# Setting the order of instructions anew: a matmul's weight load counted apart, other priorities

## The chip, the core and the metric

The kernel runs on one core of one Trainium2 chip. The metric is device time in microseconds (us) of one execution. A core has engines with instruction queues of their own that run side by side and wait for one another through semaphores: TensorE (PE, with its weight loads listed apart as PEld), VectorE (DVE), ScalarE (ACT), GpSimd (POOL), and SyncE (SP), which here does nothing but issue DMAs. Within one queue instructions run in the order in which they were written. That order is what the change touches.

## The reference

One layer of an encoder trunk, for a prompt of 1024 tokens and a sample of 32 tokens, all in float32, model width 1024:

- `u = rmsnorm(h) @ w_in` gives q, k, v and a gate for two groups (A, B) of 8 heads of width 64 each.
- Group A is softmax attention with a relative-position bias, over the query's own chunk of 64 positions and the 8 chunks before it. Group B is "stick-breaking" attention: weight `exp(log_sigmoid(z) + sum of log_sigmoid(-z) over the later keys)`, strictly causal. The sample's queries also see a cache of 512 keys and values.
- `y = concat(oA * silu(gA), oB * silu(gB)) @ w_out`, then `h = h + rmsnorm(y)`, then `h = h + sigmoid(h @ w_ple_gate) * (p @ w_ple)`.
- Outputs are both results and the new keys and values.

## The kernel before

**Work.** Each float32 operand of a matrix product is split into a high and a low part (names ending in h and l), and a product is three matmuls: high by high, high by low, low by high. `mm_*` are the input projections: 32 column blocks (q, k, v and the gate g, groups A and B, four pairs of heads), each in 3 chunks of 352 tokens and 24 matmuls per chunk. `S*` are attention scores, `ptw*` transposes of the attention weights on PE, `PV*` weights times values; a name with a small s (`SsB`, `PVsB`, `KhsB`) belongs to the sample. `ple` is `p @ w_ple`. `o0P` to `o3P` and `g0P` to `g3P` are the two closing 1024x1024 products, done by a scheme of seven block products; `o` and `g` with 64 weight columns are the sample's share of them.

**Stages.** Stage 0 is the norm and the first projections; stages 1 to 8 each mix the attention of one pair of heads with the projections of the next pair (stage 8: the gates); stage 9 is the late part of `ple`; stages 10 to 13 are the closing products.

**Buffers.** A column block's raw weights come by DMA into tiles with the tag `wr`, of which there are 4 (two per block); ACT casts them to `wh`, POOL subtracts to get `wl`. The same 4 rooms with tag `wr` also hold the sample's keys and values (`Kh`, `Kl`, `Vh`, `Vl`), so a weight load can have to wait until the sample's matmuls have read them. SP issues all DMAs from one queue.

**What sets the order.** The program does not write its instructions as the code runs. `Recorder` keeps each one as an `Op` with what it depends on; at the end `emit` (called on the last line of `stream_step`) asks `order` for one sequence and writes it. `order` runs `simulate`, a list scheduler: each engine takes, of the ops that are ready, the one with the lowest rank, and a time that `cost` estimates from the op's size passes. After each run, `latest` goes backward from the end and gives each op a due time, the latest moment at which it could start. The next run ranks by due time. In the last of the 9 passes an op's own priority is added:

```
            out, end = self.simulate(lambda o: (o.key[0], o.index + last * o.shift, o.index) if o.eng == "PE" and not PE_LATEST else (0, o.due + last * 10 * o.shift, o.index))
```

The priority, `o.shift`, is the sum of two table entries: `AHEAD_OF[engine, kind]` and `AHEAD_AT[stage, engine, kind]`, where the kind is the first letters of the written tile's name up to a digit, an A, a B or an underscore (`wr_kA2` gives `wr`, `SsB0` gives `Ss`, `wlS1o2` gives `wlS`). It is multiplied by 10 and added to a due time in ns: +100 puts an op 1 us later in the ranking, -100 1 us earlier. It changes only the order in which ready ops are taken, and no data.

For PE, `cost` before gives a transpose 109 ns (62 ns for at most 64 rows) and a matmul the larger of 109 ns and 2.5 + 0.449 ns for each streamed column. `MARGIN` (400 ns) is what the scheduler adds to whatever PE waits for from another engine. For a DMA it adds `DMA_START` (1850 ns), the transfer at `DMA_RATE` or by its pieces, and `DMA_MARGIN` (2100 ns).

All engine calls pass through one helper, so nearly every row of the profile has the line 781; tiles' names tell them apart.

Of the kernel before, what the change touches and what calls it, by code (L numbers as in the profile page):

```python
# [28 lines left out]
    ('ACT', ''): -307, ('ACT', 'L'): -414, ('ACT', 'Qfs'): -110, ('ACT', 'Qhs'): -859,  # L29
    ('ACT', 'S'): -381, ('ACT', 'be'): 32, ('ACT', 'g'): 244, ('ACT', 'gT'): -473,  # L30
    ('ACT', 'hnh'): 1092, ('ACT', 'kd'): 363, ('ACT', 'newh'): -483, ('ACT', 'o'): -50,
    ('ACT', 'om'): -5, ('ACT', 'p'): -1128, ('ACT', 'sq'): 108, ('ACT', 'stk'): 127,
    ('ACT', 'stq'): -682, ('ACT', 'wh'): -79, ('ACT', 'whS'): -249, ('ACT', 'xS'): -955,
    ('ACT', 'xb'): -149, ('ACT', 'yb'): -199, ('DVE', ''): -1363, ('DVE', 'Kl'): 290,
    ('DVE', 'L'): 377, ('DVE', 'R'): 818, ('DVE', 'S'): 18, ('DVE', 'Ss'): -133,
    ('DVE', 'Vh'): -402, ('DVE', 'cc'): 216, ('DVE', 'diags'): -224, ('DVE', 'gT'): 610,
    ('DVE', 'h'): 1157, ('DVE', 'hnl'): 253, ('DVE', 'lg'): -586, ('DVE', 'newl'): 326,
    ('DVE', 'o'): 347, ('DVE', 'ot'): -72, ('DVE', 'over'): 1049, ('DVE', 'sgg'): 302,
# [3 lines left out]
    ('PE', 'ptxs'): 7, ('POOL', 'be'): 315, ('POOL', 'bias'): 960, ('POOL', 'g'): 573,  # L42
    ('POOL', 'ksS'): 1098, ('POOL', 'om'): -712, ('POOL', 'r'): -536, ('POOL', 'sgg'): 1213,
# [5 lines left out]
}  # L49
AHEAD_AT = {  # L50
    (0, 'ACT', 'hnh'): -902, (0, 'ACT', 'pleo'): 783, (0, 'ACT', 'sq'): 26, (0, 'ACT', 'v'): -215,
    (0, 'PE', 'mm'): -297, (0, 'PE', 'ple'): 252, (0, 'POOL', 'wl'): -634, (0, 'SP', 'wpr'): 528,
    (0, 'SP', 'wr'): -232, (0, 'SP', 'x'): -74, (1, 'ACT', 'ot'): -442, (1, 'ACT', 'wTh'): 589,
    (1, 'ACT', 'wh'): 43, (1, 'DVE', 'S'): 928, (1, 'DVE', 'om'): 258, (1, 'DVE', 'wTl'): 279,
    (1, 'PE', 'S'): -86, (1, 'SP', 'sum'): -1097, (2, 'ACT', 'L'): 674, (2, 'ACT', 'be'): -112,
    (2, 'ACT', 'ot'): -548, (2, 'ACT', 'vt'): 555, (2, 'ACT', 'wTh'): 152, (2, 'DVE', 'om'): 60,
    (2, 'DVE', 'vt'): 389, (2, 'PE', 'S'): 43, (2, 'SP', 'o'): 677, (2, 'SP', 'sum'): 621,
    (3, 'ACT', 'Qfs'): 130, (3, 'ACT', 'stq'): 1238, (3, 'ACT', 'wh'): 323, (3, 'DVE', 'L'): -248,
    (3, 'DVE', 'Vh'): 390, (3, 'DVE', 'Vl'): 233, (3, 'DVE', 'diags'): 564, (3, 'DVE', 'om'): 40,
    (3, 'DVE', 'ot'): 169, (3, 'DVE', 'over'): 620, (3, 'DVE', 'vt'): 997, (3, 'DVE', 'vx'): 1005,  # L60
# [3 lines left out]
    (4, 'ACT', 'stq'): 92, (4, 'ACT', 'wTh'): -49, (4, 'DVE', 'Kl'): 168, (4, 'DVE', 'S'): 37,  # L64
    (4, 'DVE', 'Vl'): 530, (4, 'DVE', 'newl'): -393, (4, 'DVE', 'om'): -78, (4, 'DVE', 'v'): 323,
# [3 lines left out]
    (5, 'ACT', 'stv'): 620, (5, 'ACT', 'wTh'): 828, (5, 'ACT', 'wh'): 111, (5, 'DVE', 'S'): 706,  # L69
# [13 lines left out]
    (8, 'ACT', 'om'): -708, (8, 'ACT', 'ot'): -106, (8, 'ACT', 'sgg'): -442, (8, 'ACT', 'wTh'): 312,  # L83
    (8, 'DVE', 'Kcs'): -163, (8, 'DVE', 'Kl'): 236, (8, 'DVE', 'S'): 304, (8, 'DVE', 'Vl'): 1322,
# [7 lines left out]
    (11, 'ACT', 'g'): 533, (11, 'ACT', 'junk'): 705, (11, 'ACT', 'x'): 430, (11, 'ACT', 'xS'): 262,
    (11, 'DVE', 'h'): -403, (11, 'PE', 'o'): -12, (12, 'ACT', 'gT'): -495, (12, 'ACT', 'x'): -260,
    (12, 'DVE', 'gT'): -1415, (12, 'DVE', 'gj'): 887, (12, 'POOL', 's'): -859, (12, 'SP', 'hh'): 748,
    (13, 'ACT', 'x'): -379, (13, 'DVE', 'S'): 55, (13, 'DVE', 'cc'): 684, (13, 'DVE', 'wlS'): -69,
    (13, 'PE', 'g'): 217,
# [148 lines left out]
class Op:  # L245
    __slots__ = ("pieces", "eng", "what", "args", "kw", "key", "busy", "late", "ready", "left", "after", "at", "size", "shared", "table", "start", "shift", "due", "size_", "index", "users", "tiles", "old")
# [12 lines left out]
BANKS = {'mm': 1, 'S': 2, 'T': 1, 'PV': 1}  # L259
PASSES = 9  # L260
PE_LATEST = True


class Pool:
    def __init__(self, rec, stack, tc, kw):
        self.rec, self.kw, self.stack, self.tc, self.real = rec, kw, stack, tc, None
        self.psum = kw.get("space") == bass.MemoryType.PSUM
        self.tags, self.ops, self.opened = {}, [], None

    def open(self):  # L270
        self.real = self.stack.enter_context(self.tc.tile_pool(**self.kw))

# [146 lines left out]
class Recorder:  # L419
# [149 lines left out]
    def latest(self, end):  # L569
# [16 lines left out]
        while done < len(self.ops):  # L586
# [19 lines left out]
            if e != "CTL":  # L606
                free[e] = ends[o.index]
# [1669 lines left out]
```

## Time and profile before

| what | value |
|---|---|
| median of 3 runs | 767.75 us (766.9 to 767.9) |
| profiled execution: span from first to last instruction | 765.7 us |
| what lies around the span: median less span | about 2.0 us |
| PE busy | 755.8 us (99%), 4410 matmuls |
| PEld (weight loads) busy | 699.5 us (91%) |
| DVE busy | 615.7 us (80%) |
| ACT busy | 525.1 us (69%) |
| POOL busy | 447.7 us (58%) |
| DMA | 173.73 MB, mean 227 GB/s |
| granted TensorE clock, mean | 1.000 |

The profile gives no separate total time for the profiled execution, only its span; the 2.0 us is the difference between the runs' median and it. PE's busy time is the union of its matmuls from start to modelled end, and neighbours overlap, so a mean duration in a row is longer than what a matmul takes from the one before it to the one after it. That pace is read from the chain of waits, where "x24" with a length says how long 24 matmuls in a row took.

### The profile page before, as it was taken

How to read it: one execution, taken by the hardware profiler on the slowest of the kernel's cores; microseconds unless marked ns; L12 is line 12 of the kernel's file. 1: busy time of each engine (PE TensorE's matmuls, PEld its weight loads, DVE VectorE, ACT ScalarE, POOL GpSimd, SP SyncE). 2: the span in 40 equal slices, each digit the busy share in tenths (PEclk: the TensorE clock that was granted, in tenths of full speed). 3: DMA queues.
4: the chain of work that ended last, by engine and by line, in shares of the span. 5: the costliest groups of instructions: out<-in, count | busy, mean ns of one | idle time of the engine just before them, and what ended most of it. 6: DMA issues, size and time to landing. Idle time of an engine off the chain costs nothing.

```text
span 765.7 us, 14211 instructions
## 1 busy us (share of the span) xinstructions
PE 755.8 (99%) x4410; PEld 699.5 (91%) x4410; DVE 615.7 (80%) x1067; ACT 525.1 (69%) x1122; POOL 447.7 (58%) x503
## 2 busy tenths in 40 slices
PE   9999999999999999999999999999999999999997
PEld 7999999999998999999999999999998877888786
DVE  7837878898879999989798898887455688988985
ACT  6647767787766768876977786764337877784561
POOL 5623626953257555566772566778552449698453
PEclk9999999999999999999999999999999999999999
DMA  8748888778878849988878889995798856868846
GB/s 305 238 132 208 240 192 261 211 198 232 218 194 233 226 119 241 257 247 254 228 195 250 219 215 229 247 271 159 240 288 271 264 185 203 325 180 256 296 144 204
DMA packets 202525, 173.73 MB, mean 227 GB/s; under 512 B 67009, under 2 KB 164649, under 8 KB 202450
## 3 DMA queue, kind: packets, MB, share of 16 engines
q1 hardware_dynamic: 202450, 172.83, 78.7%
q8 instruction: 35, 0.57, 0.3%
q14 instruction: 40, 0.33, 0.1%
HBM read 105.72 MB, written 58.91 MB: 215 GB/s over the span
## 4 chain that ended last, share of the span: by engine, by line
PE 86%; DMA 5%; DVE 3%; ACT 2%; issue 1%; SPq 1%; POOL 0%; ACTq 0%; DVEq 0%; POOLq 0%
PE mm_vA L781 6%; PE mm_kB L781 6%; PE mm_qA L781 6%; PE mm_gA L781 6%; PE mm_gB L781 6%; PE mm_kA L781 6%; PE mm_qB L781 5%; PE PVB L781 4%; PE SA L781 3%; PE ple L781 3%; PE SB L781 3%; PE PVA L781 3%; PE o3P L781 3%; PE o1P L781 3%; PE g1P L781 3%; PE g0P L781 3%
## 5 line engine op out<-in xcount | busy, mean ns | idle before, releaser
L781 POOL TENSOR_TENSOR be<-be 128x256 f32<-128x256 f32 (+8 forms) x66 | 84.7, 1290 | 47.6 <-ACT be L781 17.8
L781 DVE TENSOR_TENSOR_SCAN be<-be,SB 128x384 f32<-128x384 f32 (+5 forms) x96 | 91.8, 962 | 12.0 <-ACT be L781 5.6
L781 ACT ACTIVATE be<-SB 128x384 f32<-128x384 f32 (+5 forms) x192 | 85.2, 499 | 18.2 <-DVE be L781 9.1
L781 DVE TENSOR_TENSOR wTl<-be,wTh 128x640 fp32r<-128x640 f32 (+2 forms) x48 | 58.6, 1228 | 4.5 <-ACT wTh L781 3.6
L781 DVE STREAM_TRANSPOSE be<-be 128x640 f32<-128x640 f32 (+3 forms) x56 | 47.7, 865 | 5.4 <-DMA be<-in_cache_b_k_dram 2.7
L781 ACT ACTIVATE be<-be,statA 128x640 f32<-128x640 f32 (+3 forms) x64 | 44.4, 695 | 10.2 <-DVE statA L781 10.0
L781 ACT CAST wTh<-be 128x640 fp32r<-128x640 f32 (+2 forms) x48 | 37.5, 785 | 4.3 <-DMA be<-swapB 2.9
L781 POOL TENSOR_TENSOR gB<-gB,gB 128x256 f32<-128x256 f32 x32 | 26.4, 845 | 18.5 <-DMA gB<-in_w_ple_gate_dram 18.5
L781 POOL TENSOR_TENSOR oB<-oB,oB 128x256 f32<-128x256 f32 x32 | 26.3, 837 | 12.7 <-DMA oB<-in_w_out_dram 10.7
L781 PE MATMUL SB<-kdB,LB 128*128 128x384 f32 (+5 forms) x96 | 33.0, 348 | 0.0
L781 PE MATMUL SB<-klB,LB 128*128 128x384 f32 (+5 forms) x96 | 33.0, 345 | 0.0
L781 DVE CUSTOM_DVE_ANT_0 be<-SA,biasA 128x320 f32<-128x320 f32 (+2 forms) x64 | 29.4, 481 | 4.0 <-PE SA L781 3.1
L781 PE MATMUL SA<-kdA,LA 128*128 128x320 f32 (+2 forms) x96 | 30.5, 322 | 0.0
L781 PE MATMUL SA<-klA,LA 128*128 128x320 f32 (+2 forms) x96 | 30.1, 317 | 0.0
L781 ACT CAST wTh<-ptwB 128x512 fp32r<-128x512 f32 (+3 forms) x48 | 22.4, 485 | 10.2 <-PE PVB L781 5.6
L781 DVE TENSOR_TENSOR wTl<-ptwB,wTh 128x512 fp32r<-128x512 f32 (+3 forms) x48 | 25.2, 543 | 3.8 <-ACT wTh L781 3.6
L781 PE MATMUL ptwB<-ident,be 128*128 128x128 f32 x144 | 26.7, 273 | 1.1 <-DVE be L781 0.7
L781 POOL TENSOR_TENSOR klA<-stkA,kdA 64x1024 fp32r<-64x1024 f32 (+2 forms) x9 | 19.9, 2215 | 10.9 <-ACT kdA L781 10.8
L781 DVE TENSOR_TENSOR LA<-stqA,LA 64x1024 fp32r<-64x1024 f32 (+2 forms) x9 | 16.7, 1857 | 10.4 <-ACT LA L781 10.2
L781 DVE TENSOR_TENSOR wTl<-ptwA,wTh 128x128 fp32r<-128x128 f32 (+3 forms) x48 | 22.1, 480 | 3.6 <-ACT wTh L781 3.4
L781 POOL TENSOR_TENSOR h<-h,x 128x512 f32<-128x512 f32 (+1 forms) x18 | 23.4, 1320 | 1.3 <-DVE h L781 1.3
L781 PE MATMUL PVB<-wTh,v2B 128*128 128x512 f32 (+1 forms) x96 | 24.1, 344 | 0.0
(694 smaller groups left out, 2652.3 us busy)
## 6 DMA issues: line engine op xcount, KB each, us to landing
swapA<-be SPq DMA_DIRECT2D x24, 320.0 KB, 3.8
be<-swapA SPq DMA_DIRECT2D x96, 80.0 KB, 2.5
oB<-in_w_out_dram SPq DMA_DIRECT2D x16, 256.0 KB, 4.5
sum_dro<-oB SPq DMA_DIRECT2D x16, 256.0 KB, 3.2
gB<-in_w_ple_gate_dram SPq DMA_DIRECT2D x16, 256.0 KB, 4.3
sum_drg<-gB SPq DMA_DIRECT2D x16, 256.0 KB, 3.3
x<-in_x_prompt_dram SPq DMA_DIRECT2D x16, 256.0 KB, 4.5
h_dr<-h SPq DMA_DIRECT2D x8, 512.0 KB, 4.5
```

The costliest lines, as they stand in the source:

```text
L781: getattr(getattr(tc.nc, o.what[0]), o.what[1])(*args, **kw)
```

## The change

Three things change, all in what sets the order; no instruction's shape, operand or engine is edited.

1. The cost of a PE op is now its stream alone, 3.5 + 0.4444 ns per column (a transpose: per row of its input), with a weight load of its own, `ldw`, 0.84 ns per weight column (107.5 ns for 128). In `simulate` a matmul starts no earlier than its own `ldw` after the start of the matmul before it; `latest` does the same backward.
2. A rule is added that, when the load of the op picked would not be hidden, looks for another ready op. Its condition asks that the other op's rank be below the picked one's plus `REACH`, and `REACH` is -1e9, while ranks are due times in ns of a program under 1e6 ns long. The passes go from 9 to 7, and the first pass's rank is written as one number.
3. Both priority tables are replaced as a whole. Some entries of the old are gone, many are new, and the largest are larger: the extremes go from about 1500 to about 11800.

The diff, with the tables cut to entries that the prediction speaks of:

```diff
 AHEAD_OF = {
...
-    ('ACT', 'om'): -5, ('ACT', 'p'): -1128, ('ACT', 'sq'): 108, ('ACT', 'stk'): 127,
-    ('ACT', 'stq'): -682, ('ACT', 'wh'): -79, ('ACT', 'whS'): -249, ('ACT', 'xS'): -955,
...
-    ('PE', 'PVs'): -797, ('PE', 'S'): -13, ('PE', 'Ss'): 29, ('PE', 'g'): -731,
...
-    ('POOL', 'ug'): -306, ('POOL', 'w'): 1007, ('SP', 'Kcs'): -173, ('SP', 'be'): -36,
...
-    ('SP', 'swap'): -38, ('SP', 'to kt'): -281, ('SP', 'wpr'): -498, ('SP', 'wr'): -45,
...
+    ('DVE', 'wTl'): -113, ('DVE', 'wl'): -499, ('DVE', 'wlS'): 11801, ('PE', 'PVs'): -716,
+    ('PE', 'Ss'): -2427, ('PE', 'g'): 335, ('PE', 'o'): -60, ('PE', 'ptp'): 518, ('PE', 'ptxs'): -364,
...
+    ('SP', 'Kcs'): 293, ('SP', 'be'): -397, ('SP', 'g'): -1115, ('SP', 'hh'): -929, ('SP', 'kl'): -653,
...
 AHEAD_AT = {
...
-    (4, 'SP', 'Kcs'): 79, (4, 'SP', 'bias'): 406, (4, 'SP', 'o'): -439, (4, 'SP', 'vs'): -1467,
-    (4, 'SP', 'wr'): -239, (5, 'ACT', 'be'): -5, (5, 'ACT', 'om'): 123, (5, 'ACT', 'ot'): -1367,
...
-    (13, 'ACT', 'x'): -379, (13, 'DVE', 'S'): 55, (13, 'DVE', 'cc'): 684, (13, 'DVE', 'wlS'): -69,
...
+    (4, 'ACT', 'om'): 290, (4, 'ACT', 'vt'): 1686, (4, 'ACT', 'wTh'): 180, (4, 'ACT', 'wh'): 787,
...
+    (4, 'PE', 'S'): 8, (4, 'PE', 'ptw'): -9, (4, 'POOL', 'om'): 417, (4, 'SP', 'Kcs'): -805,
+    (4, 'SP', 'wr'): -789, (5, 'ACT', 'be'): 73, (5, 'ACT', 'stv'): -3106, (5, 'ACT', 'wTh'): 343,
...
+LOAD = 0.84
+REACH = -1e9
+SHORT = 70.0
...
-PASSES = 9
-PE_LATEST = True
+PASSES = 7
...
+        if eng == "PE":
+            o.ldw = LOAD * args[1].shape[-1]
...
             if method == "transpose":
-                return (109 if args[1].shape[0] > 64 else 62), 165
-            return max(109.0, 2.5 + 0.449 * args[2].free()) * (1 if args[2].buf.dtype == F32R else 4), 165
+                return 3.5 + 0.4444 * args[1].shape[0], 165
+            return (3.5 + 0.4444 * args[2].free()) * (1 if args[2].buf.dtype == F32R else 4), 165
...
-        out, end = self.simulate(lambda o: o.key)
+        out, end = self.simulate(lambda o: (0, o.key[0] * 1e7 + o.index, o.index))
...
-            out, end = self.simulate(lambda o: (o.key[0], o.index + last * o.shift, o.index) if o.eng == "PE" and not PE_LATEST else (0, o.due + last * 10 * o.shift, o.index))
+            out, end = self.simulate(lambda o: (0, o.due + last * 10 * o.shift, o.index))
...
             ends[o.index] = t + o.busy
+            if e == "PE":
+                ends[o.index] = max(ends[o.index], free[e] + loads)
+                loads = o.ldw
...
+            if e == "PE":
+                if o.ldw > begun[1]:
+                    held = [x for x in now[e] if self.ops[x[1]].ldw <= begun[1] and x[0][1] < ranks[o.index][1] + REACH]
+                elif o.ldw <= SHORT and o.busy > SHORT:
+                    held = [x for x in now[e] if self.ops[x[1]].busy <= SHORT < self.ops[x[1]].ldw and x[0][1] < ranks[o.index][1] + REACH]
+                else:
+                    held = []
+                if held:
...
+                t = max(t, begun[0] + o.ldw)
+                begun = t, o.busy
```

More of the change, by code (lines that the diff above doesn't have):

```diff
@@ L35 @@
[L35 to L38, printed above, removed]
[3 rows of a table removed]
-    ('PE', 'ptxs'): 7, ('POOL', 'be'): 315, ('POOL', 'bias'): 960, ('POOL', 'g'): 573,
-    ('POOL', 'ksS'): 1098, ('POOL', 'om'): -712, ('POOL', 'r'): -536, ('POOL', 'sgg'): 1213,
[5 rows of a table removed]
+    ('ACT', 'Qfs'): 1088, ('ACT', 'g'): 1834, ('ACT', 'h'): -1086, ('ACT', 'hnh'): -120,
@@ new lines @@
+    ('ACT', 'kd'): 429, ('ACT', 'newh'): 999, ('ACT', 'o'): -2101, ('ACT', 'oT'): -4320,
+    ('ACT', 'om'): -198, ('ACT', 'ot'): -399, ('ACT', 'p'): 4138, ('ACT', 'php'): -103,
+    ('ACT', 'pleo'): 91, ('ACT', 'sgg'): -2156, ('ACT', 'sq'): 118, ('ACT', 'stq'): -597,
+    ('ACT', 'stv'): 443, ('ACT', 'v'): -402, ('ACT', 'vt'): -1313, ('ACT', 'wTh'): -13,
+    ('ACT', 'x'): -289, ('ACT', 'xS'): -152, ('DVE', 'Kcs'): 317, ('DVE', 'Kl'): 3817,
+    ('DVE', 'L'): -68, ('DVE', 'Qls'): 1342, ('DVE', 'Vh'): 1210, ('DVE', 'diags'): 115,
@@ L49 @@
+    ('DVE', 'h'): 5659, ('DVE', 'om'): -23, ('DVE', 'ot'): -714, ('DVE', 'v'): 527, ('DVE', 'vt'): -530,
+    ('DVE', 'wTl'): -113, ('DVE', 'wl'): -499, ('DVE', 'wlS'): 11801, ('PE', 'PVs'): -716,
+    ('PE', 'Ss'): -2427, ('PE', 'g'): 335, ('PE', 'o'): -60, ('PE', 'ptp'): 518, ('PE', 'ptxs'): -364,
+    ('POOL', 'Qfs'): 1837, ('POOL', 'ksS'): -2511, ('POOL', 'sgg'): -2536, ('POOL', 'wl'): 301,
[4 rows of a table added]
 }
 AHEAD_AT = {
-    (0, 'ACT', 'hnh'): -902, (0, 'ACT', 'pleo'): 783, (0, 'ACT', 'sq'): 26, (0, 'ACT', 'v'): -215,
@@ L52 @@
[L52 to L57, printed above, removed]
@@ L92 @@
[L92 to L96 removed]
+    (0, 'ACT', 'sq'): -9, (0, 'DVE', 'hnl'): 9233, (0, 'PE', 'ple'): 7969, (0, 'POOL', 'ksS'): 2989,
[5 rows of a table added]
@@ new lines @@
+    (2, 'ACT', 'stv'): 5037, (2, 'ACT', 'wTh'): -148, (2, 'DVE', 'L'): 57, (2, 'DVE', 'ot'): -1366,
+    (2, 'DVE', 'wTl'): -427, (2, 'PE', 'S'): -130, (2, 'PE', 'mm'): -48, (2, 'SP', 'be'): 950,
+    (2, 'SP', 'kl'): 193, (3, 'ACT', 'stq'): 1246, (3, 'ACT', 'stv'): -758, (3, 'DVE', 'S'): -370,
+    (3, 'DVE', 'om'): -54, (3, 'DVE', 'v'): -1037, (3, 'DVE', 'vt'): 282, (3, 'PE', 'PV'): 105,
+    (3, 'SP', 'o'): -386, (3, 'SP', 'stv'): -2397, (3, 'SP', 'swap'): 3207, (4, 'ACT', 'newh'): -752,
+    (4, 'ACT', 'om'): 290, (4, 'ACT', 'vt'): 1686, (4, 'ACT', 'wTh'): 180, (4, 'ACT', 'wh'): 787,
@@ new lines @@
+    (4, 'DVE', 'Kcs'): -344, (4, 'DVE', 'L'): 153, (4, 'DVE', 'Vh'): -865, (4, 'DVE', 'diags'): -295,
+    (4, 'DVE', 'om'): 83, (4, 'DVE', 'ot'): 628, (4, 'DVE', 'v'): -735, (4, 'DVE', 'wTl'): 152,
+    (4, 'PE', 'S'): 8, (4, 'PE', 'ptw'): -9, (4, 'POOL', 'om'): 417, (4, 'SP', 'Kcs'): -805,
+    (4, 'SP', 'wr'): -789, (5, 'ACT', 'be'): 73, (5, 'ACT', 'stv'): -3106, (5, 'ACT', 'wTh'): 343,
+    (5, 'DVE', 'over'): -2272, (5, 'DVE', 'v'): -1980, (5, 'DVE', 'wTl'): 92, (5, 'PE', 'S'): 160,
[3 rows of a table added]
+    (6, 'ACT', 'wTh'): 364, (6, 'ACT', 'wh'): 866, (6, 'DVE', 'S'): 56, (6, 'DVE', 'om'): -145,
@@ new lines @@
+    (6, 'DVE', 'ot'): -1225, (6, 'DVE', 'wTl'): -131, (6, 'PE', 'mm'): 55, (6, 'PE', 'ptw'): 32,
+    (6, 'POOL', 'g'): 5779, (6, 'SP', 'be'): -219, (6, 'SP', 'g'): 1299, (6, 'SP', 'wr'): -3261,
+    (7, 'ACT', 'be'): -292, (7, 'ACT', 'om'): -2195, (7, 'ACT', 'stk'): 4624, (7, 'DVE', 'Kcs'): 1767,
[7 rows of a table added]
+    (8, 'POOL', 'be'): 391, (8, 'POOL', 'ogg'): -1306, (8, 'POOL', 'om'): -1128, (8, 'SP', 'Kcs'): -549,
+    (8, 'SP', 'be'): -908, (8, 'SP', 'ogg'): 239, (8, 'SP', 'over'): 292, (8, 'SP', 'wr'): 119,
@@ L97 @@
+    (9, 'ACT', 'php'): 443, (9, 'ACT', 'ple'): -1755, (9, 'ACT', 'x'): 400, (9, 'PE', 'ple'): -133,
[3 rows of a table added]
 }
@@ L245 @@
 class Op:
-    __slots__ = ("pieces", "eng", "what", "args", "kw", "key", "busy", "late", "ready", "left", "after", "at", "size", "shared", "table", "start", "shift", "due", "size_", "index", "users", "tiles", "old")
+    __slots__ = ("pieces", "eng", "what", "args", "kw", "key", "busy", "late", "ready", "left", "after", "at", "size", "shared", "table", "start", "shift", "due", "size_", "index", "users", "tiles", "old", "ldw", "kind")
 LAND = {"PE": 165, "ACT": 0, "DVE": 0, "POOL": 0, "SP": 0, "CTL": 0}
@@ L459, in node @@
         o.key = (self.cls if eng == "PE" else self.low, len(self.ops), len(self.ops))
-        o.shared, o.table, o.shift, o.busy, o.late = False, None, 0, 0, 0
+        o.shared, o.table, o.shift, o.busy, o.late, o.ldw, o.kind = False, None, 0, 0, 0, 0, None
         self.ops.append(o)
@@ L496, in add @@
         o.shift = AHEAD_OF.get(kind, 0) + AHEAD_AT.get((self.stage, *kind), 0)
+        o.kind = (self.stage, *kind)
         o.busy, o.late = self.cost(eng, method, args, kw, writes, reads)
+        if eng == "PE":
+            o.ldw = LOAD * args[1].shape[-1]
         if eng == "SP":
@@ L581, in latest @@
         soon, now, free = {e: [] for e in names}, {e: [] for e in names}, dict.fromkeys(names, 0.0)
-        port, done = 0.0, 0
+        port, done, loads = 0.0, 0, 0.0
         for o in self.ops:
@@ L709, in leave @@
                 come(new.place, b.gone)
-        out, port, line, table, landed, last = [], 0.0, 0.0, AF.Exp, [], 0.0
+        out, port, line, table, landed, last, begun = [], 0.0, 0.0, AF.Exp, [], 0.0, (0.0, 1e9)
         while len(out) < len(self.ops):
@@ L735, in simulate @@
                     o = self.ops[pick[1]]
+            if e == "PE":
[6 more added lines that the diff above has]
+                if held:
+                    heapq.heappush(now[e], (ranks[o.index], o.index))
+                    pick = min(held)
+                    now[e].remove(pick)
+                    heapq.heapify(now[e])
+                    o = self.ops[pick[1]]
+                t = max(t, begun[0] + o.ldw)
+                begun = t, o.busy
             if e == "CTL":
```

21 lines of the change are left out of this document (removed), and 41 rows, old and new, of tables (AHEAD_AT, AHEAD_OF).

## The prediction

> **What bounds the kernel now.** I read the page first, for the busiest engine.
>
> ```profile
> span 765.7 us, 14211 instructions
> PE 755.8 (99%) x4410; PEld 699.5 (91%) x4410; DVE 615.7 (80%) x1067; ACT 525.1 (69%) x1122; POOL 447.7 (58%) x503
> ```
>
> PE is busy 99% of the span. A new order can take away PE's idle time and, if the order of shapes matters, PE's own work. So the second view is busy time by stretches, cut around PE's gaps (columns: PE, PEld, DVE, ACT, POOL busy with instruction counts, clock, DMA share, GB/s).
>
> ```profile
> 0.00:8.00 8.00, 6.70 (x27) 6.19 (x28) 5.44 (x7) 3.29 (x5) 2.95 (x12) 1.00 0.64 209
> ...
> 110.00:116.00 6.00, 5.47 (x36) 5.03 (x35) 5.14 (x9) 4.71 (x12) 2.57 (x3) 1.00 0.87 256
> ...
> 225.00:240.00 15.00, 13.45 (x81) 12.38 (x80) 12.25 (x20) 9.56 (x23) 9.93 (x13) 1.00 0.91 216
> ...
> 265.00:272.00 7.00, 6.10 (x33) 5.06 (x32) 6.52 (x11) 6.05 (x18) 3.99 (x5) 1.00 0.55 136
> ...
> 340.00:347.00 7.00, 6.53 (x42) 5.83 (x41) 5.17 (x10) 4.87 (x13) 6.33 (x10) 1.00 0.65 154
> ...
> 580.00:757.00 177.00, 177.00 (x770) 140.36 (x769) 141.14 (x205) 120.23 (x245) 106.84 (x102) 1.00 0.74 242
> 757.00:765.70 8.70, 3.69 (x28) 3.35 (x26) 4.71 (x10) 1.73 (x4) 2.51 (x2) 0.97 0.31 113
> sum 765.70, PE 755.79 PEld 699.46 DVE 615.71 ACT 525.10 POOL 447.73; mean PE 62.98 PEld 58.29 DVE 51.31 ACT 43.76 POOL 37.31
> ```
>
> Idle in all: 765.70 - 755.79 = 9.91 us. Of this 8.00 - 6.70 = 1.30 is before the first matmul and 8.70 - 3.69 = 5.01 after the last; both hang on the first memset and on the last product's way out, which no ranking shortens. The middle has 9.91 - 1.30 - 5.01 = 3.60 us, nearly all in four stretches: 0.53, 1.55, 0.90 and 0.47. The closing products (580 to 757) have none. Who ends those waits:
>
> ```profile
> PE PVA L781 <- ACT wTh L781: 1.0, 1, 1.0
> PE mm_vA L781 <- ACT wh_vA L781: 0.9, 1, 0.9
> PE ptwB L781 <- DVE be L781: 0.7, 2, 0.5
> PE mm_kA L781 <- ACT wh_kA L781: 0.5, 1, 0.5
> PE ptwB L781 <- ACT be L781: 0.3, 1, 0.3
> ```
>
> Six waits, 3.4 us, none over 1.0. The chain of waits shows what stands behind the two longest stretches (start, length, what).
>
> ```profile
> 224.03 5.85 DMA wr_kA<-in_w_in_dram
> ...
> 229.90 0.63 ACT wh_kA L781
> ...
> 235.65 0.61 ACT wh_qA L781
> 236.25 0.63 ACT wTh L781
> ...
> 236.93 0.79 PE PVA L781 x3
> ...
> 263.65 1.00 PE SsB L781 x8
> 264.66 0.10 PE SB L781
> 264.76 4.08 DMA wr_vA<-in_w_in_dram
> ...
> 268.86 0.63 ACT wh_vA L781
> ...
> 269.53 0.59 PE mm_vA L781 x2
> ```
>
> The second is plain: the load of `wr_vA` goes out 0.1 us after PE has done the sample's scores `SsB`, whose operands hold rooms of the tag `wr`; 4.08 us later it has landed and PE has run dry. The first begins with a weight load too, `wr_kA`, which goes out late and lands 5.85 us later; the work that piled up on ACT and POOL behind it then keeps `wTh` from `PVA`.
>
> **The change part by part.**
>
> *Counting stream and load apart.* This is worth something if PE's own time depends on which matmul stands beside which. Paces from the chain of waits:
>
> ```profile
> 206.08 0.11 PE ptwA L781
> ...
> 256.78 0.44 PE ptwB L781 x4
> ...
> 544.60 32.99 PE mm_gB L781 x205
> ...
> 593.46 2.72 PE o1P L781 x12
> ...
> 629.71 5.53 PE o L781 x24
> ```
>
> A 352-column matmul takes 32.99/205 = 161 ns, one of 512 columns 2.72/12 = 227 ns. A transpose takes 0.44/4 = 110 ns in a run of four, and 0.11 us also when it stands alone between 352-column matmuls. So a long neighbour doesn't make it cheaper. The planner's new constants say the same: its stream of 60 ns is followed by a load of 107.5 ns that the next matmul has to wait for; the old ones said 109 ns. The difference of 1.5 ns over the transposes
>
> ```profile
> L781 PE MATMUL ptwB<-ident,be 128*128 128x128 f32 x144 | 26.7, 273 | 1.1 <-DVE be L781 0.7 <-ACT be L781 0.3
> L781 PE MATMUL ptwA<-ident,be 128*128 128x128 f32 x120 | 23.3, 273 | 0.0
> ```
>
> is 264 x 1.5 = 0.4 us of planned time, and the chip does the same work as before. Only a lighter load next to a short stream would save time, and the 64-column loads (`o`, at 629.71 above, still 5.53/24 = 230 ns each) come when the attention's transposes are over:
>
> ```profile
> L781 PE MATMUL ptwB<-ident,be x144: 270/272/330, 110.4 to 541.0; 128*128 128x128 f32 x144
> ```
>
> I take 0 us, with bounds of 0 and -0.4.
>
> [...] If the load after a transpose could go out before the transpose starts, a transpose among long matmuls would cost its stream of some 60 ns, and the sum would be lower by 264 x 50 ns = 13 us. The single `ptwA` at 0.11 us says that it does not happen here.
>
> *The rule on loads.* With `REACH` at -1e9 it would need a rank a billion ns lower than the lowest ready one. It never acts: 0 us.
>
> *Passes, first rank.* They change where the due times settle, not any cost: 0 us, bounds inside those of the next part.
>
> *The priorities.* Every queue is ordered anew, SP's and POOL's among them, so no op keeps its neighbours for certain. What counts is the 3.60 us of middle idle time, and what the new order puts in its place. For the `SsB` stall the tables say something definite: the entry for PE's `Ss` goes from 29 to -2427, from 0.3 us late to 24.3 us early, in all stages; `wr` on SP in stage 4 goes from -45 - 239 = -284 to -789, 5.0 us earlier. Scores taken a few us sooner free the rooms sooner, and a lead of 1 us is enough against 0.9 us of wait. For the stall of 225 to 240 the signs are mixed: `wr` in stage 3 goes from -45 to 0 (0.4 us later), but SP's `Kcs` of stage 4, the cache loads just ahead of it in the queue, goes from -94 to -512 (4.2 us earlier, so out of the way), and ACT's `wh` of stage 4 from -79 to 787 (8.7 us later), behind other casts that are ready; that ACT order also puts `wTh` ahead of `wh_qA`, which is what `PVA` waited for (235.65 above). I count both as gone: -1.55 - 0.90 = -2.45 us. That is what PE's rows show as idle; the weight loads of the same three waits stood longer, since a matmul's modelled end covers the first part of a gap:
>
> ```profile
> PEld PVA L781 <- ACT wTh L781: 1.3, 1, 1.3
> PEld mm_vA L781 <- ACT wh_vA L781: 1.2, 1, 1.2
> PEld mm_kA L781 <- ACT wh_kA L781: 1.2, 2, 0.9
> ```
>
> Together 3.7 us, against 1.0 + 0.9 + 0.5 = 2.4 on PE. By them the gain would be 3.7, and all middle idle time, 3.60, would be up to 3.60 x 3.7/2.4 = 5.5 us. I stay at the lower value, as some new lateness will come in elsewhere. Bounds: -5.5 us, and above zero the slow rival below.
>
> **The sum.** 765.7 - 2.45 = 763.3 of span; with the 2.05 us by which the median of the runs stands above that span, 765.3 us. With all of the middle gone it would be 767.75 - 5.5 = 762.3, the floor for any order: nothing else on PE moves.
>
> **The rivals.**
>
> *The stalls move (no change, 767.7).* All six waits end on ACT or DVE work that a DMA or a chain of three engines feeds. What the planner thinks of DMAs isn't changed. For a 256 KB weight load it counts 1.85 us, its pieces and 2.1 us of margin, under 5 us; the trace has
>
> ```profile
> DMA to landing us min/median/max: 4.3/5.8/8.6
> ```
>
> for the eight `wr_kA`. So the next order has its own late loads, in other places. Speaking for it: six waits in 4410 matmuls are what is left when an order already meets the planner's times. Against: `Ss` is aimed at a wait that is there. If as much comes back as goes, 767.7 us.
>
> *The low halves come late in the closing products (slower, 769.9).* The entry for DVE's `wlS` goes from none (-69 in stage 13) to 11801, 118 us later, so DVE does every other ready op first. These are the low parts of 16 left operands, and each product of 2.72 us needs its own at the third matmul; they are made three products of a pair ahead, so some 3 x 2 x 2.72 = 16 us. PE has no idle time there, so any lateness shows at once. DVE is not far from full:
>
> ```profile
> 720.00:740.00 20.00, 20.00 (x89) 16.00 (x88) 17.82 (x27) 14.30 (x28) 12.78 (x10) 1.00 0.61 192
> ...
> L781 DVE STREAM_TRANSPOSE ug<-ht 128x1024 f32<-128x1024 f32 x4 | 9.1, 2287 | 0.0
> ...
> L781 DVE TENSOR_TENSOR wlS3g<-xS3g,whS3g 128x512 fp32r<-128x512 f32 x2 | 1.4, 684 | 0.1
> ```
>
> It decides from the point at which DVE has other ready work for 16 us on end: then the `wlS` waits behind one more transpose of 2.29 us. Once in each of the two gate sets: +4.6, with the gain of above 767.75 - 2.45 + 4.6 = 769.9 us. Against it: at 17.82 of 20 us DVE does run dry every few us, and then takes it. [...]
>
> *The load is hidden after all (faster, 754.5).* [...] The new order would have to place transposes singly, and the trace shows them at 0.11 either way.
>
> **How the numbers follow.** A measurement of this kernel tells about 0.2%, 1.5 us, from no change. Forecast (part or all of the middle gone) 0.44; stalls move 0.27; low halves late, 0.18, and other lateness of that kind, 0.10, in which a changed queue delays a load by more than the two stalls gave; load hidden 0.01. So faster 0.45, same 0.27, slower 0.28. The range goes from 762.3, the floor, to 771.5, the slow rival and a stall of 1.6 us (the 225 stretch) more; outside are 0.04 below and 0.12 above. The forecast's own range is 762.3 to 766.2.
>
> **What would show it.** Right: no wait of PE on `wh_vA` after `SsB`, middle idle time near 1.2 us, PE's busy time within 1 us of 755.8, transposes still at 0.11 us, 580 to 757 still full. The stalls moved: idle of 3 to 4 us in the middle with other names. Slow rival: PE waiting for DVE `wlS` after 590 us. Wrong altogether: a shorter busy time of PE by several us (loads hidden), or idle time in stage 0 or after the last matmul that moved.

## The result and the profile after

The changed kernel takes 771.5 us (median of 16 runs, 768.6 to 773.4), the kernel before beside it 767.7 us (16 runs, 765.0 to 770.6). The ratio is 1.0051, interval 1.0039 to 1.0063: slower by half a per cent, at the upper edge of the range and on the other side of the forecast.

The head of the page after: span, then each engine's busy time.

```profile
span 769.5 us, 14248 instructions
PE 756.2 (98%) x4410; PEld 698.3 (91%) x4410; DVE 613.5 (80%) x1067; ACT 525.0 (68%) x1122; POOL 451.4 (59%) x503
```

PE's work is what it was (756.2 us against 755.8). Of 3.8 us more span, 0.4 is busy time and 3.4 idle time: 769.5 - 756.2 = 13.3 us against 9.9. The stretches of the kernel after, cut around its own gaps (length, then busy PE, PEld, DVE, ACT, POOL, clock, DMA share, GB/s):

```profile
0.00:8.00 8.00, 5.58 (x26) 4.96 (x27) 4.65 (x6) 2.38 (x3) 2.95 (x12) 1.00 0.72 208
8.00:100.00 92.00, 91.42 (x579) 87.61 (x578) 63.52 (x130) 60.80 (x131) 47.70 (x64) 1.00 0.74 219
100.00:119.00 19.00, 17.99 (x112) 16.72 (x110) 13.27 (x21) 14.69 (x30) 8.02 (x12) 1.00 0.76 216
119.00:280.00 161.00, 161.00 (x1026) 155.78 (x1025) 145.28 (x260) 122.11 (x273) 94.86 (x113) 1.00 0.78 211
280.00:300.00 20.00, 19.57 (x125) 18.98 (x125) 18.70 (x35) 14.97 (x30) 13.17 (x8) 1.00 0.74 219
...
338.00:356.00 18.00, 15.34 (x88) 13.05 (x88) 13.56 (x21) 11.83 (x28) 7.94 (x11) 1.00 0.69 203
...
460.00:480.00 20.00, 19.33 (x120) 18.67 (x119) 18.84 (x29) 12.82 (x25) 15.24 (x15) 1.00 0.87 221
480.00:580.00 100.00, 99.48 (x624) 97.19 (x623) 62.57 (x104) 49.04 (x109) 67.28 (x68) 1.00 0.81 230
580.00:757.00 177.00, 177.00 (x774) 140.77 (x773) 140.25 (x207) 122.73 (x250) 107.24 (x103) 1.00 0.75 242
757.00:769.50 12.50, 7.47 (x45) 6.41 (x43) 6.80 (x13) 2.44 (x5) 3.81 (x3) 0.90 0.45 155
```

In the kernel before, the stretch 119 to 280 had the two stalls that the prediction counted as gone:

```profile
119.00:280.00 161.00, 158.52 (x1003) 152.17 (x1002) 141.52 (x253) 118.50 (x264) 93.54 (x112) 1.00 0.78 209
338.00:356.00 18.00, 17.53 (x109) 16.53 (x108) 15.80 (x25) 12.78 (x31) 13.54 (x16) 1.00 0.80 236
```

They are gone: 161.00 of 161.00, where 2.48 us were idle. The closing products (580 to 757) are full as before, and the end costs 12.50 - 7.47 = 5.03 us, before 5.01. But the middle now has new idle time: 0.58 + 1.01 + 0.43 + 2.66 + 0.67 + 0.52 = 5.87 us in place of 3.60, and the start 2.42 in place of 1.30. The longest of PE's waits after (the first matmul's wait for `newh`, 1.3 us, stands in the kernel before too):

```profile
PE ptwB L790 <- POOL be L790: 2.0, 2, 1.5
PE idle L790 <- DVE newh L790: 1.3, 1, 1.3
PE ptp L790 <- DMA pp<-in_p_prompt_dram: 1.1, 1, 1.1
PE ptwB L790 <- ACT be L790: 0.9, 2, 0.7
PE PVA L790 <- DVE be L790: 0.7, 1, 0.7
PE ple L790 <- ACT php L790: 0.6, 1, 0.6
```

The waits for `wTh` and for the two weight casts of before are not among them. The largest gap, 338 to 356, begins in SP's queue. Its rows (start, length, transfer), then the chain of waits:

```profile
337.86 0.40 SPq L790 DMA_DIRECT2D wr_vA<-in_w_in_dram  x1
338.35 0.53 SPq L790 DMA_DIRECT2D klB<-klB  x1
338.97 0.54 SPq L790 DMA_DIRECT2D wr_vA<-in_w_in_dram  x1
339.56 1.03 SPq L790 DMA_DIRECT2D gB<-in_w_ple_gate_dram  x1
340.68 1.11 SPq L790 DMA_DIRECT2D o_dr<-otA  x2
```

```profile
341.24 4.26 DMA o_dr<-otA
...
345.60 0.96 DVE over L790
346.57 0.43 DVE otA L790
347.03 0.42 DVE wTl L790
347.46 0.74 DVE be L790
```

Two stores of `otA` stand behind four other transfers. Until the second has landed, at 345.5 us, the room that the next `otA` needs is taken, so ACT waits 2.3 us, and the casts and exponentials of group B that follow on ACT wait with it. DVE's `over`, a reciprocal, needs a room of the same tag and waits for the same store. PE's row at the end of the gap:

```profile
346.64 0.30 PE L790 MATMUL ptwB<-ident,be 128*128 128x128 f32 x1 [1.54 <-POOL be L790]
```

The row puts the wait down to POOL, but POOL's `be` had ended 0.7 us earlier. What ended just before was `over` (at 346.55): it reads `ptr`, and the program takes `ptr` and `ptwB`, both written by PE, from the same tag `T` of its pool `ps`. PE starts this `ptwB` 0.09 us after `over` ends in the trace of the changed kernel, and 0.10 us after it in those of after_start_stores and after_scan, so the path from the store to PE goes through `over`. The entries for SP's `wr` in stage 6 went from -45 + 687 = 642 to -3261, 39 us earlier in the ranking; the two `wr_vA` loads in front of the stores fit that.

### The profile page after: what moved, and what is told of

Read it like the earlier page. It is cut to its first block, busy times and chain, and to the rows that moved or that the text cites. A ratio compares the mean times of both kernels' runs of the same rounds, so it can differ in the third digit from the quotient of the medians.

```text
span 769.5 us, 14248 instructions
## 1 busy us (share of the span) xinstructions
PE 756.2 (98%) x4410; PEld 698.3 (91%) x4410; DVE 613.5 (80%) x1067; ACT 525.0 (68%) x1122; POOL 451.4 (59%) x503
## 4 chain that ended last, share of the span: by engine, by line
PE 51%; DMA 4%; DVE 3%; issue 2%; ACT 1%; POOL 1%; SPq 1%; POOLq 0%; ACTq 0%; DVEq 0%
PE mm_gB L790 6%; PE mm_gA L790 5%; PE o1P L790 3%; PE g0P L790 3%; PE o2P L790 3%; PE o0P L790 3%; PE g2P L790 3%; PE o3P L790 3%; PE g1P L790 3%; PE g3P L790 2%; PE PVB L790 2%; PE ple L790 2%; DVE be L790 2%; PE mm_kB L790 2%; PE mm_vA L790 2%
## 5 line engine op out<-in xcount | busy, mean ns | idle before, releaser
L790 POOL TENSOR_TENSOR be<-be 128x512 f32<-128x512 f32 (+8 forms) x66 | 84.4, 1283 | 64.0 <-ACT be L790 29.9
L790 PE MATMUL SA<-kdA,LA 128*128 128x320 f32 (+3 forms) x96 | 30.5, 321 | 0.0
L790 PE MATMUL SA<-klA,LA 128*128 128x320 f32 (+3 forms) x96 | 29.8, 315 | 0.0
L790 POOL TENSOR_TENSOR klB<-stkB,kdB 64x1024 fp32r<-64x1024 f32 x8 | 20.5, 2566 | 8.8 <-ACT kdB L790 8.4
L790 PE MATMUL PVB<-wTl,v2B 128*128 128x512 f32 (+1 forms) x96 | 24.4, 347 | 0.0
L790 PEld LDWEIGHTS ptwB<-ident,be 128*128 128x128 f32 x144 | 18.5, 140 | 6.1 <-POOL be L790 2.7
```

What stands on the lines that cost most here:

```text
L790: getattr(getattr(tc.nc, o.what[0]), o.what[1])(*args, **kw)
```

## The experiments

All ratios are to the kernel before, run beside on the same chip. It took 765.9 to 766.4 us there, against 767.7 us beside the changed kernel above, so times in us of different groups are not to be compared; the ratios are. An idle time is that of one profiled execution, and executions of one kernel differ by up to 5.6 us (765.0 to 770.6 above), so a verdict is taken from the ratio where the two disagree (the profiled execution of after_stores has a span of 765.4 us, under that of the kernel before, and its median is 770.2 us).

### Are the late transfers the cause? after_start, after_stores, after_start_stores, after_scan

Each writes the planner's sequence with a few ops moved, and nothing else (`put` takes ops out of the sequence and writes them ahead of a given op, or with `True` behind it; `find` names them by engine and tile):

```diff
 # after_start, after_start_stores, after_scan
+    pp = find("SP", "pp0")
+    put(pp[1:], pp[0], True)
 # after_stores, after_start_stores, after_scan
+    stores = find("SP", "otA20_1_0") + find("SP", "otA20_1_1")
+    late = find("SP", "wr_vA3_0") + find("SP", "klB21") + find("SP", "wr_vA3_1") + find("SP", "gB221")
+    put([o for o in late if out.index(o) < out.index(stores[1])], stores[1], True)
 # after_scan
+    put(find("DVE", "omB20_4", "SB20_4_1"), find("DVE", "wTlA21_1", "beA21_5")[0])
+    put(find("DVE", "omB20_4", "SB20_4_0"), find("DVE", "over2")[0])
```

> The changed kernel with one DMA moved in SP's queue: the second half of pp goes out right behind the first, as before the change, and no longer behind grow and the first quarter of wpr. Theory A (the new stalls are single late transfers in SP's queue, each worth what PE waits for it): the 1.1 us of PE waiting on pp and most of the 0.6 us on php go, so 771.5 - 1.7 = 769.8 us, 1.003 of the kernel before. Theory B (the loss is spread over the whole attention part, as an order that counts PE too fast; early lateness is made up for before the next stall): idle time moves behind 8 us and the time stays at 771.5 us, 1.005.

> The changed kernel with four loads of SP's queue (two of wr_vA, one klB copy, one gB) moved behind the two stores o_dr<-otA that they stood ahead of at 338 us. Theory A: the stores go out some 3 us earlier, ACT's 2.3 us wait for a room of the tag ot falls under 0.5, PE's idle time in 338 to 356 falls from 2.7 to about 0.7, and the time to 769.5 us, 1.0025 of the kernel before. Theory B: the attention chain over ACT, DVE and POOL is late there anyway, PE's idle time in 338 to 356 stays over 2 us and the time at 771.5 us.

> Both moves in one kernel. Theory A: the gains add up, 771.5 - 1.7 - 2.0 = 767.8 us, 1.000 of the kernel before. Theory B: 771 to 771.5 us.

> Edit on the changed kernel: the two moves of after_start_stores, and on DVE the two prefix scans omB20_4 go ahead of the 128x640 wTl and of the reciprocal over2, which ran for 1.73 and 0.94 us in front of them at 341.9 us. Theory A (the idle left in 338 to 356, 1.49 us, is DVE's order: the attention chain waits for these scans for 2.1 us): the first scan starts near 341.9 instead of 345.3 us, the idle of the stretch falls to 0.5 or less, and the span by 1 us against 767.8; the ratio to the kernel before near 1.003. Theory B (the chain is short by as much at its next link): the idle stays at 1.2 us or more with PE waiting for something else, ratio unchanged at 1.004.

Measured: 769.4 us, 1.0043 (1.0026 to 1.0059); 770.2 us, 1.0051 (1.0032 to 1.0070); 769.5 us, 1.0040 (1.0027 to 1.0054); 768.6 us, 1.0024 (1.0010 to 1.0039). The wait on `pp` goes, and that of `ple` on `php` grows from 0.6 to 1.0 us. In after_stores the stretch 338 to 356 has 1.48 us idle instead of 2.66, and the time shows nothing of it; in after_start, which doesn't move the stores, it has 1.78. With both moves ACT no longer waits for the stores. With the scans ahead as well, the stretch is no fuller:

```profile
338.00:356.00 18.00, 16.51 (x95) 14.28 (x94) 14.66 (x22) 12.32 (x29) 9.41 (x11) 1.00 0.70 221
```

```profile
338.00:356.00 18.00, 16.04 (x98) 14.85 (x98) 14.19 (x22) 12.19 (x28) 9.94 (x12) 1.00 0.68 214
```

```profile
345.38 0.30 PE L810 MATMUL ptwB<-ident,be 128*128 128x128 f32 x1 [1.33 <-POOL be L810]
```

```profile
342.12 0.82 DVE L810 TENSOR_TENSOR_SCAN be<-be,SB 128x320 f32<-128x320 f32 x1 [0.40 <-issue]
342.85 0.80 DVE L810 TENSOR_TENSOR wTl<-be,wTh 128x640 fp32r<-128x640 f32 x1
...
344.36 0.92 DVE L810 RECIPROCAL over<-ptr 16x128 f32<-16x128 f32 x1
```

(The first row is the stretch in after_start_stores, the second in after_scan; then PE's row and DVE's rows of after_scan.) Idle falls from 2.66 to 1.49 us, then stands at 1.96. The scan runs at 342.1 instead of 345.3 us, but `over` now starts at 344.36 instead of 343.52, and PE starts again 0.10 us after its end; POOL's `be`, which the row names, had ended 0.6 us before. The move of the scans put two of them ahead of the row that PE was waiting for. An order with `over` itself ahead was not run. So the store is a real link of that gap, but not its only one, and the span of after_scan is the same 767.8 us.

Of the theories, after_start decides nothing, as its interval holds the values of both; the time of after_stores is theory B's, its idle time lies between the two; after_start_stores rules out theory A's 1.000, and the idle time of after_scan is theory B's. With all three moves the ratio falls from 1.0051 to 1.0024 (1.0010 to 1.0039), about half of the 0.5%, with intervals that just touch. No one place is shown to carry it.

### Were the first stalls to be had at all? before_wk, before_wth, before_start

Three single moves on the kernel before:

```diff
 # before_wk: four cache loads behind the two late weight loads, on SP
+    loads = find("SP", "wr_kA2_0") + find("SP", "wr_kA2_1")
+    cache = find("SP", "KcsB0")
+    put([o for o in cache if out.index(o) < out.index(loads[1])], loads[1], True)
 # before_wth: on ACT
+    put(find("ACT", "wThA11_1", "beA11_7"), find("ACT", "wh_qA2_0")[0])
 # before_start: the start of the kernel after, on SP
+    pp = find("SP", "pp0")
+    put(pp[1:], find("SP", "wpr0_0True")[0], True)
```

> The kernel before with one move: the two loads of wr_kA for the third pair of heads go out ahead of the first four cache loads (Kc) of the sample, ahead of which SP's queue had placed all but one of the cache loads. Theory A: wh_kA starts about 1.6 us earlier than 229.9 us, PE's idle time in 225 to 240 falls from 1.55 to under 0.7 us, the time to about 766.5 us, 0.9985. Rival: the cache loads are as late by then as wr_kA was, DVE's transposes of Kc hold up DVE's queue about 1 us longer, PE's wait moves onto that, and the time stays at 767.7 us.

> Edit on the kernel before: on ACT the cast wThA11_1 goes ahead of the cast wh_qA2_0, nothing else. It is the order that the prediction named for the first stall (PVA waited 1.01 us for wTh, whose 0.63 us stood behind a wh_qA of 0.61 us). Theory A (the wait is that order): PE's wait for wTh falls from 1.0 to 0.4 us, the idle of 225 to 240 from 1.55 to 0.95, time 0.6 us lower, ratio 0.999. Theory B (the stall moves): wh_qA or a later cast is awaited instead, idle of 225 to 240 within 0.2 of 1.55, ratio 1.000 to 1.002.

> The kernel before with the changed kernel's fault at the start: the second half of pp goes out behind the first quarter of wpr. Theory A (a late transfer costs what PE waits for it): PE waits about 1.1 us on pp and 0.5 on php, and the time goes up by 1.1 to 1.7 us to 768.8 to 769.4, 1.0015 to 1.002. Theory B (early lateness is made up for): 767.7 us.

Measured: 767.0 us, 1.0013 (1.0001 to 1.0026); 765.6 us, 0.9986 (0.9969 to 1.0003); 767.1 us, 1.0015 (1.0002 to 1.0028). With the weight load 2 us earlier, the cast `wh_kA` runs 2 us earlier, and the stretch 225 to 240 is no fuller (15.00 - 13.20 = 1.80 us idle, before 1.55). The stretch, PE's longest wait and the chain in before_wk:

```profile
225.00:240.00 15.00, 13.20 (x80) 12.42 (x79) 12.19 (x20) 9.58 (x22) 10.25 (x12) 1.00 0.77 197
```

```profile
PE PVA L796 <- ACT wTh L796: 1.3, 1, 1.3
```

```profile
226.76 3.22 DMA be<-in_cache_b_k_dram
230.06 0.06 DVE be L796
```

The cache load that was moved back is now the late one, and the chain goes through DVE, as the rival said. With `wTh` ahead on ACT, its wait does fall from 1.0 to 0.5 us and the stretch has 15.00 - 14.44 = 0.56 us idle, while a later stretch is emptier (7.00 - 5.02 = 1.98 us, before 0.47). The two stretches in before_wth:

```profile
225.00:240.00 15.00, 14.44 (x85) 13.12 (x85) 12.79 (x20) 9.23 (x23) 10.54 (x13) 1.00 0.93 231
...
340.00:347.00 7.00, 5.02 (x32) 4.24 (x31) 3.72 (x8) 4.54 (x13) 6.26 (x10) 1.00 0.62 159
```

0.9986 cannot be told from no change. A single stall of 1 us can be moved away; none of these moves shows a gain on the total. The start of the kernel after costs the kernel before 0.15% (0.02 to 0.28%), about the 1.3 us that PE waits for `pp` in before_start; theory A's price fits.

### Model or priorities? before_ss, model_only, tables_only

```diff
 # before_ss: the kernel before with one entry
-    ('PE', 'Ss'): 29
+    ('PE', 'Ss'): -2427
 # model_only: the code after with the two tables of before
 # tables_only: the code before with the two tables of after
```

> The kernel before with one entry of the tables changed, PE's Ss from 29 to -2427 as in the new tables. By the prediction's reading (an entry acts on its own kind of work and on what waits for it): the wait of 0.9 us at wh_vA goes, the rest stays, 766.8 us. By the rival (one entry moves the rest of the order as well, so an entry can't be priced alone): other waits of PE appear, 3 to 15 us slower.

> The new counting of PE's time and the 7 passes, with the old priorities. If the counting is worth something by itself (shorter PE work): PE busy below 755 us and 767.7 us or less. If it is worth nothing and the priorities only fit the planner's timeline that they were set for: PE busy within 1 us of 755.8, several new waits of PE, and slower than the kernel before by 5 to 20 us.

> The new priorities with the old counting and the 9 passes. If the new priorities carry the loss or gain of the change by themselves: about 771.5 us. If priorities only fit the timeline that they were set for: several new waits of PE, 5 to 20 us slower than the kernel before, PE busy within 1 us of 755.8.

Measured: 776.7 us, 1.0138 (1.0112 to 1.0164); 781.6 us, 1.0217 (1.0187 to 1.0246); 790.7 us, 1.0322 (1.0302 to 1.0343). Each half alone costs four to six times what the pair costs, so the two can't be priced apart and added. In before_ss the rival holds: the entry brings waits in other places and no gain. PE's busy time was expected within 1 us of 755.8 and is 761.0 and 764.1 us in model_only and tables_only, and tables_only is 5 us slower than the worst that was expected. That a table must fit its planner is not shown by before_ss and model_only, whose ratios lie inside the spread that orders without any table have below (up to 1.0217); only tables_only lies outside it. PE's longest waits in tables_only:

```profile
PE mm_kB L767 <- ACT wh_kB L767: 3.0, 1, 3.0
PE PVB L767 <- DVE v2B L767: 2.6, 1, 2.6
PE SA L767 <- DVE statA L767: 1.9, 2, 1.4
```

### Without any priorities: notables_old, notables_new

```diff
+AHEAD_OF, AHEAD_AT = {}, {}
```

in the kernel before and in the changed one.

> The kernel before with both tables of priorities empty, so that every op is ordered by its due time alone. Both theories: slower than with the tables, ratio between 1.01 and 1.06. It is there for the comparison with notables_new.

> The changed kernel with both tables empty: the new counting and the passes without any priorities. Theory A (the counting itself is worth nothing, as PE's own work does not depend on the neighbours; it only needs a fitting table): within 1% of notables_old, on either side, and PE's busy time within 1% of it with transposes at 0.11 us. Theory B (the new counting gives a truer order): faster than notables_old by 1% or more, with PE's busy time lower, not only its waits.

Measured: 767.2 us, 0.9999 (0.9986 to 1.0013), and 770.3 us, 1.0053 (1.0035 to 1.0070). This was the surprise: each kernel without its tables is as fast as with them, and the 0.5% is still there. The tables of neither kernel show a gain. Both theories had expected notables_old to be slower by 1% or more. Of the two, theory A holds (within 1% of each other, and the new one is not the faster), but that leaves open what makes the 0.5%.

### The counting, the passes, or the draw? nt_old_pass7, nt_old_pass8, nt_old_tr108, nt_new_pass8, nt_new_pass9, nt_new_load107

A draw here means one order out of the many that the planner can come to; a change of any constant in it makes another. All these runs have empty tables; `nt_old` is the code before, `nt_new` the code after. One constant each:

```diff
 # nt_old_pass7, nt_old_pass8
-PASSES = 9
+PASSES = 7          # or 8
 # nt_old_tr108
-                return (109 if args[1].shape[0] > 64 else 62), 165
+                return (108 if args[1].shape[0] > 64 else 62), 165
 # nt_new_pass8, nt_new_pass9
-PASSES = 7
+PASSES = 8          # or 9
 # nt_new_load107
-LOAD = 0.84
+LOAD = 0.836
```

> The kernel before, both tables empty, 7 passes over the due times instead of 9, nothing of the new counting. Theory A (every change of the order is a new draw, and 0.5% is the spread of such draws): anywhere in 0.997 to 1.008 of the kernel before. Theory B (the new counting itself gives the worse order): 0.998 to 1.002, as notables_old at 0.9999. Theory C (two passes fewer do it): 1.004 to 1.007, as notables_new at 1.0053.

> The kernel before, both tables empty, 9 passes, the planner's cost of a 128-column transpose 108 ns instead of 109 and nothing else: a change without meaning, which still puts 1917 of PE's 4410 matmuls in another place of its order. Theory A (spread of draws): 0.997 to 1.008. Theories B and C: 0.998 to 1.002.

> The changed kernel, both tables empty, 9 passes instead of 7: the new counting alone. Theory A (spread of draws): 0.997 to 1.008. Theory B (the counting): 1.004 to 1.007. Theory C (the passes): 0.998 to 1.002.

> The changed kernel, both tables empty, 8 passes: a second draw with the new counting. Theory A: 0.997 to 1.008, and its distance from nt_new_pass9 may be as large as 0.3%. Theory B: 1.004 to 1.007, as nt_new_pass9 and notables_new, within 0.2% of each other. Theory C: between the two.

> The kernel before, both tables empty, 8 passes: a fourth draw with the old counting, after 0.9999, 1.0072 and 1.0204. Theory A (the time is the luck of one order, the counting has no part in it): anywhere in 0.999 to 1.021, so that the mean of the four old ones and that of the four new ones differ by less than their spread. Theory B (the new counting is the worse by 0.5%): at 1.000, which would put the old ones apart from the new ones but for the two odd draws.

> The changed kernel, both tables empty, the weight load of a 128-column operand counted at 107.0 ns instead of 107.5: again a change without meaning, which puts 2611 of PE's 4410 matmuls in another place of its order. Theory A: anywhere in 0.999 to 1.021, as the old ones. Theory B: 1.004 to 1.008.

| empty tables | ratio, interval | span | PE busy | PE idle |
|---|---|---|---|---|
| old counting, 9 passes (notables_old) | 0.9999 (0.9986 to 1.0013) | 765.4 | 756.0 | 9.4 |
| old, 8 passes | 1.0055 (1.0037 to 1.0073) | 770.6 | 757.1 | 13.5 |
| old, 7 passes | 1.0072 (1.0052 to 1.0092) | 771.9 | 757.6 | 14.3 |
| old, transposes 108 ns | 1.0204 (1.0187 to 1.0220) | 781.2 | 760.2 | 21.0 |
| new counting, 7 passes (notables_new) | 1.0053 (1.0035 to 1.0070) | 768.5 | 756.6 | 11.9 |
| new, 8 passes | 1.0060 (1.0040 to 1.0080) | 771.0 | 757.8 | 13.2 |
| new, 9 passes | 1.0141 (1.0116 to 1.0167) | 777.8 | 759.3 | 18.5 |
| new, load 107.0 ns | 1.0217 (1.0178 to 1.0256) | 781.6 | 762.0 | 19.6 |

One nanosecond in 109 in the planner's cost of a transpose moves the time by 2%; half a nanosecond in 107.5 by 1.6% against notables_new; one pass fewer by 0.55%. Theory A's range of 0.997 to 1.008 was too narrow for nt_old_tr108 and nt_new_pass9, and 1.021 for nt_new_load107; nt_new_pass8 and nt_new_pass9 lie 0.8% apart where it allowed 0.3%. Its mechanism fits all six. Theory B needed nt_old_pass7 and nt_old_tr108 within 0.2% of 1.000, theory C needed nt_old_tr108 and nt_new_pass9 there: both fall. The four old draws have a mean of (0.9999 + 1.0055 + 1.0072 + 1.0204) / 4 = 1.008, the four new ones (1.0053 + 1.0060 + 1.0141 + 1.0217) / 4 = 1.012, and each four spread by 0.8% (standard deviation). The difference of 0.35% has an uncertainty of 0.8% times the root of 1/4 + 1/4, or 0.6%. So the counting has no effect that these runs show. With four draws a side, and those chosen by hand, an effect from about -1% to +2% stays open. What is shown is that 0.5% lies well inside what any change of the planner's constants does, good or senseless.

## Why the prediction was wrong, point by point

*What bounds the kernel: right.* PE bounds the two kernels and the eight orders with empty tables. Their idle time is 9.4 to 21.0 us, and the ratio rises with it, but for the last two (21.0 us at 1.0204, 19.6 us at 1.0217).

*Counting apart, 0 us, bounds 0 and -0.4: right as a price of instructions, wrong as a term of the sum.* The matmuls' work did not move (756.2 against 755.8, within the 1 us that was named). A transpose still costs 0.11 us (0.55/5) after the change:

```profile
307.81 0.55 PE ptwA L790 x5
...
373.00 0.55 PE ptwB L790 x5
```

But the edit also deals all queues anew. With empty tables and 9 passes, the counting alone gave +1.4% (nt_new_pass9 against notables_old). A change of 1 ns in the cost of a transpose, less than the 1.5 ns that the prediction multiplied by 264 to get 0.4 us, gave +2.0%, 16 us. *The passes, 0 us, failed in the same way:* 9 to 7 alone gave +0.7%. *The rule on loads* was not run by itself.

*The priorities, -2.45 us: the mechanism came, the sum did not.* The two stalls are gone from 119 to 280 us, 2.48 us in all, and no wait on `wh_vA` after `SsB` is left. The failed step is the next sentence of the prediction, "I stay at the lower value, as some new lateness will come in elsewhere": that lateness was counted at zero. Its sum left 3.60 - 2.45 = 1.15 us idle in the middle; 5.87 were measured, so 4.72 us of new waits, and 1.12 us more at the start. With 0.4 us more busy time, -2.45 + 4.72 + 1.12 + 0.4 = 3.8 us, which is the growth of the span. What the runs show in place of the zero is the spread of the orders: 0 to 2.2% with empty tables. Which of the three parts of the change made this draw stays open. Whether the table entries named there (`Ss`, `wr`, `Kcs`, `wh`) brought the gain is not shown: `Ss` alone, in the old code, cost 1.4%, and without tables the changed kernel takes the same time.

*The rivals.* "The stalls move" was the right mechanism with the wrong price, for it said that as much comes back as goes; the prediction's 0.10 for "a changed queue delays a load by more than the two stalls gave" is nearest to what came, though the largest new gap began with a late store. The low halves were not late: no wait for `wlS`, 580 to 757 full. "Load hidden" is out by the 0.11 us above: nothing measured here shows the 50 ns a transpose, 13 us in all, that it was priced at. The start moved by 1.12 us, which the prediction had named as a sign that it was wrong altogether; it is one of several new waits and not the largest part.

*The range.* Its upper edge, 771.5 us, is the result, by luck: it was worked out from late low halves, which did not come, and one stall of 1.6 us, while the kernel shows several new waits of up to 1.5 us. The floor of 762.3 us was not reached: no order that was run has a ratio under 0.9986. One reading behind it is off: the 1.2 us of `mm_kA` on PEld are two waits, the longer 0.9, against one wait on PE. With 1.3 + 1.2 + 0.9 = 3.4 us in place of 3.7 the floor would be 762.6.

## What to carry to other kernels

When a list scheduler writes a whole program, every edit of its costs, passes or priorities is a new draw from all its orders, and the draw decides more than the edit means. Before pricing an edit, measure the spread with senseless ones (a cost 1% off, one pass fewer): here it is 0.8% over eight orders, so a single order 0.5% slower says next to nothing on the idea behind it. An order that already has only 3.6 us idle in the middle is near the good end of the draws seen here: seven of the eight with empty tables were slower by 0.5% or more. Listing the waits that an edit removes gives one side of the sum only; the other side is what other orders of the same kernel show as idle time.

## What the hardware showed

*Waits of PE with a lower clock behind them.* In nt_old_tr108, PE waits 2.91 us for DVE, and from 382 to 386 us its granted clock is 0.66 and then 0.50. Two waits of that execution, and the stretches that follow them (columns as above; the clock is the third number from the end):

```profile
209.67 0.84 PE L782 MATMUL PVA<-wTl,v2A 128*128 128x512 f32 x4 [2.58 <-DVE wTl L782]
...
381.09 1.55 PE L782 MATMUL mm_qA<-hnh,wh_qA 128*128 128x352 f32 x8 [2.91 <-DVE be L782]
```

```profile
210.00:212.00 2.00, 2.00 (x15) 1.81 (x14) 1.94 (x3) 1.98 (x4) 2.00 (x2) 1.00 0.29 111
...
380.00:382.00 2.00, 0.91 (x6) 0.92 (x7) 1.93 (x6) 1.46 (x4) 0.71 (x4) 1.00 0.90 246
382.00:384.00 2.00, 2.00 (x11) 1.98 (x11) 1.05 (x2) 2.00 (x5) 1.29 (x2) 0.66 0.81 133
384.00:386.00 2.00, 2.00 (x10) 1.93 (x9) 1.89 (x3) 1.15 (x2) 1.09 (x1) 0.50 0.60 146
386.00:388.00 2.00, 2.00 (x14) 2.00 (x13) 2.00 (x3) 1.53 (x4) 1.82 (x4) 0.99 0.74 189
```

By the clock, an estimated 2.00 x (0.34 + 0.50 + 0.01) = 1.7 us are lost again, as busy time: six matmuls of 352 columns take 1.91 us there (from 383.34 us), and eight take 1.29 us right behind (from 386.24 us). The same execution has a second such stretch (348 to 352 us, clock 0.62 and 0.52) after a wait of 2.25 us. By the same estimate that is 2.00 x (0.38 + 0.48) = 1.7 us more, so the two would be 3.4 of the 4.2 us by which PE's busy time in this execution is above that of notables_old (760.2 against 756.0). nt_new_pass9 has a clock of 0.94 from 300 to 320 us and of 0.91 from 500 to 520 us, with 2.60 and 3.06 us of PE idle in them, and of 1.00 from 260 to 280 us, with 2.81 us idle. In the kernel before and in the changed one no stretch of 2 us up to 756 us has a clock under 1.00; there it plays no part. In nt_old_tr108 waits of 2.25 and 2.91 us had a lower clock behind them, while the one of 2.58 us was followed by a clock of 1.00, so the length of a single wait does not decide it.

*A DVE instruction of 0.80 us took 4.85.* PE's wait of 2.91 us is for a DVE row that stands behind it in the queue. DVE's row, then POOL's:

```profile
375.38 4.85 DVE L782 TENSOR_TENSOR wTl<-be,wTh 128x640 fp32r<-128x640 f32 x1
```

```profile
375.14 2.39 POOL L782 TENSOR_TENSOR klA<-stkA,kdA 64x1024 fp32r<-64x1024 f32 x1
377.47 0.13 POOL L782 MEMSET be<- 128x1 f32 x2
377.56 1.99 POOL L782 TENSOR_TENSOR be<-be 128x1024 f32<-128x1024 f32 x1
```

The same shape took 0.80 us in after_scan (342.85 above). Here it ends 0.7 us after POOL's second long instruction, as if it had waited for both. Rows of this shape in the kernel before agree: one that began at 193.01 us, while a long row of POOL ran, took 2.52 us and ended 0.7 us after that row, and one at 204.32 us with POOL idle took 0.82. That such a row of DVE waits for POOL is the author's reading of these rows, which no run tested; if it holds, DVE went on waiting when POOL passed from `klA` (to 377.53 us) to `be` (from 377.56 us). It would be one of the ways in which a new order makes new lateness: which pairs fall together is dealt anew each time.
